# One layer of a hybrid decoder on one core: time steps in four row groups, the query scale on the scores, a later table load, and early short transfers in the weights' queue

## The chip, the cores and the metric

The kernel runs on one core of one Trainium2 chip. The metric is device microseconds of one execution, the median of several runs. The engines of the core are TensorE (PE), VectorE (DVE), ScalarE (ACT), GpSimd (POOL) and SyncE (SP, which only issues transfers). A core has 16 DMA engines, fed by queues that SP, ACT and POOL issue into.

## What is computed

One inference step of one layer, in fp32, for 256 prompt tokens and 64 sample tokens (8 sequences of 8), which share all weights; the model is 2048 wide. Cut to its skeleton:

```python
x += mixer(rmsnorm(x))         # h = xn @ w_in, split into z, x/B/C, dt, sc_h, sc_b, sc_c
                               # dt = softplus(h_dt + dt_bias); a = -exp(a_log) * dt   (32 heads)
                               # x/B/C: causal conv of 4 taps, silu; ssd_scan; short conv of 3 taps
                               # out = concat(y_ssd * silu(z) normed, y_sc) @ w_out
x += mem_attend(rmsnorm(x), k, v)   # k, v = rmsnorm(mem) @ w_mem_k, w_mem_v for the prompt; cached for samples
x += peer(rmsnorm(x))
# peer: q = xn @ w_peer_q; s = q . sub_keys (8 heads, 2 halves, 128 keys)
#       top 16 of each half, top 16 of their 256 sums -> expert ids and softmax gates g
#       act = gelu(xn . u[eid]);  out = sum of g * act * v[eid]       (16384 experts)
y = rmsnorm(x)                 # and the new SSM, conv and memory states are returned
```

## The kernel before

The layer is a chain of matrix products whose weights come from HBM once. Every fp32 weight tile is split into two parts, a rounded H and the rest L (`split`, L246 to L249: ACT copies, DVE subtracts), and so are the tokens (AH, AL; BH, BL); three matmuls (AH x H, AL x H, AH x L) make one product. In the order of time: K and V of the memory tokens (`tokens_gemm`, matmuls L318 to L320), the columns of w_in (`gemm`, matmuls L371 to L373: first the 32 dt columns C_DT, then B, C, x, then the short convolution's), the z columns, w_out, attention over memory (L1196 to L1430), the query of the experts, then a sweep over all of peer_u (U stage, L1939 to L1993) and over all of peer_v (V stage, L2034 to L2146).

The order of the work on PE, ACT and DVE is the program's own order. The class `Stream` writes it: a weight unit is loaded (SP's queue, into one of four rooms of 512 KB, tiles named W), split into rings of seven H and L, and popped, which is when its matmuls are written. Side work (generators passed to `side`) takes a step after each pop, `soon(n, fn)` runs a function n pops later, and `wait(n)` lets n steps pass. The orders of SP and POOL come from a tile scheduler. A room is taken by a load, and given back when DVE has subtracted its second half. A copy of peer_u to a transposed tensor u_d in HBM goes on beside it, 1 MB at a time, in ACT's queue.

The places that are touched:

- `histories` (L537 to L551) loads, on POOL's queue at the program's start, dt_bias, a_log, the D row, and the convolutions' histories into HX, four row groups of 24 x 24 x 32 and four of 16 x 16 x 32 floats. `vectors` (L517) loads norm gains and convolution weights on SP's queue; `x_norm` (L490) normalises the tokens during the K/V stage.
- The dt columns come from `gemm(w_in[0], C_DT, NH, ...)`: four loads of 64 KB in weight rooms, eight units of six matmuls with 32 columns of PE in use. `evac_dt` adds the bias, and `delta` (L616) computes softplus by a series, on 32 partitions x 320 tokens (tiles dt, DTT, AT); after `wait(DW)`, `decays` (L647) turns DTT and AT by six transposes (`ptd`) into DN and AN, 128 tokens x 32 heads, and makes running sums (`pta`, `ptc`), their exponentials (DD) and `ptr`.
- `residual` (L1032) transposes x again in the z stage from tiles xr, and `short_in` (L1047) splits the short convolution's result from tiles ys; both load on POOL's queue.
- `norm_p` (L1549) makes rs, the reciprocal root mean square of each token, from a sum over partitions (`prs`), on all partitions and by token columns. `evac_p` (L1601) scales q by it on DVE and has ACT copy the sample columns a second time; `scores` (L1611) multiplies q with the keys (`psc` for prompt, `pscs` for samples), and ACT copies the scores to SS, from which `best_keys` (L1632 to L1640) takes the top 16 on DVE.
- In the U stage, an expert block's result `at` gets its Gelu on ACT (L1988) and goes to act_d on SP's queue. `open_v` (L2011) opens the V stage and runs a Sqrt on one column (`warm`, L2022), which makes ACT load that function's table.

Of the kernel before, what the change touches and what calls it, by code (L numbers as in the profile page):

```python
# [19 lines left out]
P = 128  # L20
# [27 lines left out]
DW, XW, LAG = 8, 5, 4  # L48
# [115 lines left out]
def step(ctx, tc, ins, outs, dbg=None, stop=None):  # L164
# [325 lines left out]
    def x_norm():  # L490
        gb = gain_rows(norm_mix[0])
        yield from wait(4)
# [44 lines left out]
    def histories():  # L537
        nc.gpsimd.dma_start(dtb, ssd_dt_bias[0].rearrange("(h o) -> h o", o=1))
        nc.gpsimd.dma_start(alog, ssd_a_log[0].rearrange("(h o) -> h o", o=1))
        heads_d = pM.tile([P, NH], F32, name="heads_d")  # L540
        nc.gpsimd.dma_start(heads_d, ssd_d[0].rearrange("(o h) -> o h", o=1).broadcast_to([P, NH]))
        G.memset(HX, 0.0)
        for c0, src, nrow, nk in ((0, state_ssd_conv, 24, 24), (768, state_short_conv, 16, 16)):
            rows = src[0].rearrange("b j (k r i) -> r (b j) k i", r=4, i=32)
            for r in range(4):
                nc.gpsimd.dma_start(HX[32 * r:32 * r + nrow, c0:c0 + 32 * nk].rearrange("c (k i) -> c k i", i=32), rows[r])
            yield 1
        for h2 in range(2):
# [67 lines left out]
    def delta(x, e, s, s2):  # L616
# [6 lines left out]
        yield 1  # L623
        V.tensor_tensor(s, s, e, ALU.mult)
        V.tensor_tensor(s2, s, s, ALU.mult)
        yield 1
        q = e
        V.tensor_scalar(q, s2, 1.0 / 17, None, op0=ALU.mult)
        for j in range(7, 0, -1):
            V.scalar_tensor_tensor(q, q, 1.0 / (2 * j + 1), s2, ALU.add, ALU.mult)  # L630
            if j % 2:
                yield 1
        V.scalar_tensor_tensor(q, q, 1.0, s, ALU.add, ALU.mult)
        V.tensor_scalar(x, x, 0.0, None, op0=ALU.max)
        yield 1
        V.scalar_tensor_tensor(DTT, q, 2.0, x, ALU.mult, ALU.add)
        V.tensor_scalar(AT, DTT, alog, -1.0, op0=ALU.mult, op1=ALU.mult)
        yield from wait(DW)
        yield from decays()

    def evac_dt(m, pt):
        d = pS.tile([P, 3, 512], F32, tag="XD", bufs=1, name="dt")[0:NH].rearrange("p a b -> p (a b)")
        d = [d[:, i * T:(i + 1) * T] for i in range(4)]
        V.tensor_scalar(d[0], pt[0:NH, 0:T], dtb, None, op0=ALU.add)
        strm.side(delta(*d), 1)

    def decays():  # L647

        pt = ps("ptd")
        for j, src in enumerate((DTT, AT)):  # L650
            for b in range(3):
                n = P if b < 2 else TS
                transpose(pt[0:n, (3 * j + b) * NH:(3 * j + b + 1) * NH], src[:, b * P:b * P + n])
        for j, dst in enumerate((DN, AN)):
            S.activation(dst[:, 0:2], pt[:, 3 * j * NH:(3 * j + 2) * NH].rearrange("p (b h) -> p b h", h=NH), AF.Copy)
            S.activation(dst[0:TS, 2], pt[0:TS, (3 * j + 2) * NH:(3 * j + 3) * NH], AF.Copy)
        yield from wait(2)
# [288 lines left out]
    gemm(w_in[0], C_DT, NH, AH, AL, T, evac_dt)  # L946
# [100 lines left out]
    def short_in():  # L1047
        for k in range(KC):
            y = pZ.tile([P, T], F32, tag="ys", bufs=3, name="ys")
            nc.gpsimd.dma_start(y, ysc_d[k])  # L1050
            split(BH[:, k], BL[:, k], y)
# [549 lines left out]
    def evac_p(m, pt, c):  # L1601
# [3 lines left out]
        V.tensor_tensor(q[:, 0:T], pt[:, 0:T], RS["p"], ALU.mult)  # L1605
        S.activation(q[:, T:T + TS], q[:, TP:T], AF.Copy)
# [4 lines left out]
    def scores(c, qs):  # L1611
# [8 lines left out]
        S.activation(PP["SS"][:, 0:2, 2 * c + 1:2 * c + 3], pt.rearrange("p (j t k) -> p t j k", t=2, k=P), AF.Copy)  # L1620
# [4 lines left out]
        S.activation(PP["SS"][:, 2, 2 * c + 1:2 * c + 3], pt[:, 0:2 * P].rearrange("p (j k) -> p j k", k=P), AF.Copy)  # L1625
# [297 lines left out]
    def u_unit(i, q):  # L1923
# [36 lines left out]
        def comp():  # L1960
# [18 lines left out]
            if q == 3:  # L1979
# [31 lines left out]
    def open_v():  # L2011
# [10 lines left out]
        S.activation(warm, ident[:, 0:1], AF.Sqrt)  # L2022
# [229 lines left out]
```

## Time and profile before

| | us |
|---|---|
| median of 3 runs | 3107.21 (3105.64 to 3111.11) |
| the profiled execution | 3115.06 |
| its span in the trace | 3113.4 |
| PE busy | 3063.9 (98%) |
| DVE busy | 2281.4 (73%) |
| ACT busy | 1588.7 (51%) |
| POOL busy | 1341.6 (43%) |

The span is the time from the first to the last instruction in the trace; 1.66 us of the profiled execution lie outside it. Busy shares are means over stages with different limits, so the places where an engine stands still are read one by one. Matmuls overlap in the records: the time of one is the distance from its start to the next one's start, not its duration. The clock column of the windows is the granted TensorE clock, 1.00 for 2.4 GHz and 0.50 for 1.2 GHz.

### The profile page before, as it was taken

Reading aid. Unit: us, or ns where it says so; the run is one execution under the profiler, and the core shown is the slowest. Engines: PE = TensorE matmul, PEld = TensorE weight load, DVE = VectorE, ACT = ScalarE, POOL = GpSimd, SP = SyncE. Lnnn points to the kernel's source line nnn. Section 1 sums busy time; section 2 is a strip of 40 time slices with the busy share of each in tenths; the row PEclk is TensorE's granted clock in tenths of the full one; section 3 lists DMA queues with packets and bytes.
Section 4 is the critical chain, followed back from the end, with each engine's and each line's share of the span. In section 5 each row is a group of like instructions: output and inputs, shape, how many; then the busy total and the mean of one; then the engine's idle time right before and its main releaser. Section 6 shows DMA issues by size and latency. Waiting matters only on the chain.

```text
span 3113.4 us, 55309 instructions
## 1 busy us (share of the span) xinstructions
PE 3063.9 (98%) x19685; PEld 2804.0 (90%) x19685; DVE 2281.4 (73%) x4500; ACT 1588.7 (51%) x3192; POOL 1341.6 (43%) x1509
## 2 busy tenths in 40 slices
PE   8999999999999999999999999999999999999998
PEld 7889999999999999889999999888888888877886
DVE  5556776666566456656888899988885878878886
ACT  5545544334454444344454444767665555544555
POOL 1011221111110002320358899988886546456543
PEclk9999999999999999999999999999999999999999
DMA  7888899899999858975866788879998999998996
GB/s 259 291 272 298 296 335 323 303 325 314 343 327 340 277 179 224 269 251 157 232 214 214 283 320 317 304 288 324 331 330 274 343 329 364 320 328 314 334 318 217
DMA packets 442025, 909.16 MB, mean 292 GB/s; under 512 B 39880, under 2 KB 248944, under 8 KB 416276
## 3 DMA queue, kind: packets, MB, share of 16 engines
q1 hardware_dynamic: 312980, 543.11, 51.3%
q0 software_dynamic: 61040, 227.77, 22.2%
q10 hardware_dynamic: 67728, 134.75, 12.7%
q8 instruction: 154, 2.52, 0.3%
q14 instruction: 123, 1.01, 0.1%
HBM read 849.41 MB, written 190.05 MB: 334 GB/s over the span
## 4 chain that ended last, share of the span: by engine, by line
PE 41%; DMA 2%; POOL 2%; DVE 2%; issue 2%; ACT 1%; DVEq 0%; SPq 0%; POOLq 0%; ACTq 0%
PE pu L1970 8%; PE acc L2145 6%; PE acc L2144 6%; PE acc L2146 6%; PE pu L1971 4%; PE pu L1977 2%; PE pu L1976 2%; PE pu L1975 2%; POOL L L1951 2%; PE pgate L1873 2%; DMA at<-act_d 1%; DMA gv<-in_peer_v_dram,EV 1%; DVE L L249 1%; PE pg L373 1%; PE pg L372 1%
## 5 line engine op out<-in xcount | busy, mean ns | idle before, releaser
L249 DVE TENSOR_TENSOR L<-W,H 128x512 fp32r<-128x512 f32 x1320 | 899.5, 706 | 367.1 <-ACT H L248 360.3
L248 ACT ACTIVATE H<-W 128x512 fp32r<-128x512 f32 x1320 | 798.2, 625 | 719.1 <-PE acc L2146 227.9
L1951 POOL TENSOR_TENSOR L<-tt,H 128x512 fp32r<-128x512 f32 x511 | 646.4, 1297 | 60.7 <-ACT H L1948 55.0
L371 PE MATMUL pg<-AH,H 128*128 128x320 f32 (+1 forms) x1872 | 587.7, 314 | 0.3 <-ACT H L248 0.3
L373 PE MATMUL pg<-AH,L 128*128 128x320 f32 (+1 forms) x1872 | 579.7, 310 | 3.2 <-DVE L L249 3.2
L372 PE MATMUL pg<-AL,H 128*128 128x320 f32 (+1 forms) x1872 | 579.3, 309 | 0.0
L2145 PE MATMUL acc<-L,wt 128*128 128x512 f32 x1024 | 400.0, 391 | 6.3 <-DVE L L249 6.3
L2144 PE MATMUL acc<-H,wt 128*128 128x512 f32 x1024 | 399.6, 390 | 2.2 <-DVE at L1984 2.2
L2146 PE MATMUL acc<-H,wt 128*128 128x512 f32 x1024 | 399.4, 390 | 0.0
L1948 ACT ACTIVATE H<-tt 128x512 fp32r<-128x512 f32 x512 | 308.8, 625 | 142.1 <-DVE tt L1939 113.0
L1939 DVE STREAM_TRANSPOSE tt<-W 128x512 f32<-128x512 f32 x512 | 337.8, 690 | 52.6 <-POOL L L1951 48.6
L1970 PE MATMUL pu<-XP,H 128*128 128x512 f32 x1035 | 371.3, 399 | 0.0
L373 PEld LDWEIGHTS pg<-AH,L 128*128 128x128 f32 (+1 forms) x1872 | 351.0, 188 | 4.8 <-DVE L L249 4.2
L371 PEld LDWEIGHTS pg<-AH,H 128*128 128x128 f32 (+1 forms) x1872 | 351.4, 188 | 3.1 <-ACT H L248 0.9
L372 PEld LDWEIGHTS pg<-AL,H 128*128 128x128 f32 (+1 forms) x1872 | 351.0, 188 | 2.4
L1971 PE MATMUL pu<-XP,L 128*128 128x256 f32 x1104 | 297.1, 279 | 0.2 <-POOL L L1951 0.2
L1977 PE MATMUL pu<-XP,L 128*128 128x256 f32 x944 | 268.9, 285 | 1.7 <-POOL L L1951 1.6
L1975 PE MATMUL pu<-XP,H 128*128 128x256 f32 x944 | 267.7, 284 | 0.0
L1976 PE MATMUL pu<-XP,H 128*128 128x256 f32 x944 | 267.0, 283 | 0.0
L2093 POOL TENSOR_TENSOR at<-at,G 128x108 f32<-128x108 f32 x192 | 151.5, 803 | 262.7 <-DMA at<-act_d 215.8
L2145 PEld LDWEIGHTS acc<-L,wt 128*128 128x128 f32 x1024 | 192.9, 188 | 47.4 <-DVE L L249 7.3
L2144 PEld LDWEIGHTS acc<-H,wt 128*128 128x128 f32 x1024 | 192.9, 188 | 42.6 <-ACT wt L248 2.6
(495 smaller groups left out, 5817.0 us busy)
## 6 DMA issues: line engine op xcount, KB each, us to landing
u_d<-in_peer_u_dram ACTq DMA_DIRECT2D x128, 1024.0 KB
W<-u_d SPq DMA_DIRECT2D x128, 1024.0 KB
W<-in_peer_v_dram SPq DMA_DIRECT2D x256, 512.0 KB
W<-in_w_in_dram SPq DMA_DIRECT2D x176, 512.0 KB
W<-in_w_out_dram SPq DMA_DIRECT2D x64, 512.0 KB
W<-in_w_mem_k_dram SPq DMA_DIRECT2D x32, 512.0 KB
W<-in_w_mem_v_dram SPq DMA_DIRECT2D x32, 512.0 KB
kv<-in_cache_mem_k_dram POOLq DMA_DIRECT2D x64, 256.0 KB
```

The lines of the kernel that those rows point to most:

```text
L248: S.activation(h, src, AF.Copy)
L249: V.tensor_tensor(l, src, h.bitcast(F32), ALU.subtract)
L371: PE.matmul(out, hv[:, j, c0:c1], ah[:, k, 0:n], start=st, stop=False)
L372: PE.matmul(out, hv[:, j, c0:c1], al[:, k, 0:n], start=False, stop=False)
L373: PE.matmul(out, lv[:, j, c0:c1], ah[:, k, 0:n], start=False, stop=sp)
L1939: V.transpose(tt.rearrange("p (k a i) -> p k a i", a=4, i=32), box["x", i].rearrange("p (a k j) -> p k a j", a=4, k=16)[:, 4 * q:4 * q + 4])
L1951: G.tensor_tensor(l, src, h.bitcast(F32), ALU.subtract)
L1970: PE.matmul(*wide, start=k == 0, stop=False)
L1971: PE.matmul(pu[:, 0:TP], lv[:, j], PP["xp"][:, 0, k], start=False, stop=False)
L2144: PE.matmul(out, th, h, start=i == 0, stop=False)
L2145: PE.matmul(out, th, l, start=False, stop=False)
L2146: PE.matmul(out, tl, h, start=False, stop=i == P - 1)
```

## The change

The history loads, dt_bias and a_log go from POOL's queue to SP's, among the K/V weights, and the 2048 x 32 dt weights are loaded there whole (WDT, 128 x 16 x 32, rows of 128 bytes). The dt columns are then one unit without weight loads or splits: 32 fp32 matmuls with unrounded weights, of which four neighbours go to different column groups of 32 (k = 4q + j to group j), so that each group holds a part of the sum. FOLD (four stacked identities) adds the four parts and turns the result in one matmul per 128 tokens. `delta` then runs on 128 x 96, and `decays` starts without transposes, two steps later instead of eight. Residual rows are loaded one tile ahead (two buffers for xr), and the short convolution's one tile ahead. The query is copied unscaled on ACT; the scale becomes a per-partition operand of the score copies, for which rs is turned into a column (`prt`). `warm` is run 12 pops later, and the last two stores to act_d go through ACT's queue.

```diff
     def histories():
-        nc.gpsimd.dma_start(dtb, ssd_dt_bias[0].rearrange("(h o) -> h o", o=1))
-        nc.gpsimd.dma_start(alog, ssd_a_log[0].rearrange("(h o) -> h o", o=1))
...
-                nc.gpsimd.dma_start(HX[32 * r:32 * r + nrow, c0:c0 + 32 * nk].rearrange("c (k i) -> c k i", i=32), rows[r])
+                nc.sync.dma_start(HX[32 * r:32 * r + nrow, c0:c0 + 32 * nk].rearrange("c (k i) -> c k i", i=32), rows[r])
...
+    def dt_unit():
+
+        pt = ps("pdt")
+        for i, a in enumerate((AH, AL)):
+            for q in range(4):
+                for j in range(4):
+                    k = 4 * q + j
+                    PE.matmul(pt[32 * j:32 * j + 32, 0:T], WDT[:, NH * k:NH * k + NH], a[:, k].bitcast(F32),
+                              start=i == q == 0, stop=i == 1 and q == 3)
+        S.activation(D4[:, 0:T], pt[:, 0:T], AF.Copy)
+        strm.side(delta(), 1)
+
+    def delta():
+
+        yield from wait(2)
+        pt = ps("ptd")
+        for b in range(3):
+            PE.matmul(pt[:, b * NH:(b + 1) * NH], D4[:, b * P:(b + 1) * P], FOLD, start=True, stop=True)
...
+        V.tensor_tensor(by_block(x), by_block(pt[:, 0:3 * NH]), rows(DTB), ALU.add)
         V.scalar_tensor_tensor(e, x, -1.0, x, ALU.mult, ALU.max)
         S.activation(e, e, AF.Exp, scale=-1.0)
+        S.activation(ALOG, ALOG, AF.Exp)
...
-    gemm(w_in[0], C_DT, NH, AH, AL, T, evac_dt)
+    strm.add(None, None, None, dt_unit)
...
     def residual():
...
+                for src in (x_prompt[0, 0:P], x_prompt[0, P:TP]) if b == 0 else (x_sample.rearrange("b l d -> (b l) d"),):
+                    xts.append(pZ.tile([P, D], F32, tag="xr", bufs=2, name="xr"))
+                    nc.gpsimd.dma_start(xts[-1][:src.shape[0]], src)
...
     def norm_p():
...
+        yield from wait(3)
+        pt = ps("prt")
+        for i in range(2):
+            PE.matmul(pt[:, i:i + 1], r[:, i * P:(i + 1) * P], ident[:, 0:1], start=True, stop=True)
+            PE.matmul(pt[TS * i:TS * i + TS, 2:3], r[:, TP:T], ident[:, 0:1], start=True, stop=True)
+        RS["t"] = PP["pool"].tile([P, 3], F32, name="rt")
+        S.activation(RS["t"], pt[:, 0:3], AF.Copy)
...
-        V.tensor_tensor(q[:, 0:T], pt[:, 0:T], RS["p"], ALU.mult)
-        S.activation(q[:, T:T + TS], q[:, TP:T], AF.Copy)
+        S.activation(q[:, 0:TP], pt[:, 0:TP], AF.Copy)
+        S.activation(q[:, TP:].rearrange("p (r t) -> p r t", r=2), pt[:, TP:T].unsqueeze(1).broadcast_to([P, 2, TS]), AF.Copy)
...
-        S.activation(PP["SS"][:, 0:2, 2 * c + 1:2 * c + 3], pt.rearrange("p (j t k) -> p t j k", t=2, k=P), AF.Copy)
+        for tb in range(2):
+            S.activation(PP["SS"][:, tb, 2 * c + 1:2 * c + 3], pt.rearrange("p (j t k) -> p t j k", t=2, k=P)[:, tb], AF.Copy,
+                         scale=RS["t"][:, tb:tb + 1])
...
-                    nc.sync.dma_start(act_d[:, i], at)
+                    (nc.scalar if i >= P - 2 else nc.sync).dma_start(act_d[:, i], at)
...
-        S.activation(warm, ident[:, 0:1], AF.Sqrt)
+        strm.soon(12, lambda: S.activation(warm, ident[:, 0:1], AF.Sqrt))
```

How the instructions stand, at three places. First, the issues of short transfers at the start. On POOL before, after the masks (dtb, alog and heads_d are the three small vectors; XS holds HX):

```order
L538 DMA dtb<-in_ssd_dt_bias_dram 32x1
L500 AFFINE_SELECT TRI<-TRI 128x128
L504 AFFINE_SELECT BDO<-BDO 64x64
L539 DMA alog<-in_ssd_a_log_dram 32x1
L506 AFFINE_SELECT BDO<-BDO 64x64
L541 DMA heads_d<-in_ssd_d_dram 128x32
L542 MEMSET XS 128x1280
L546 DMA XS<-in_state_ssd_conv_dram 24x24x32 x4
L546 DMA XS<-in_state_short_conv_dram 16x16x32 x4
```

On SP in the change, among the loads of w_mem_k (XS<-in_w_in is WDT, the last group of XS rows is HX):

```order
L440 DMA gb<-in_norm_mix_dram 128x2048
L298 DMA W<-in_w_mem_k_dram 128x2x512 x4
L520 DMA XS<-in_w_in_dram 128x16x32
L298 DMA W<-in_w_mem_k_dram 128x2x512 x2
L522 DMA XS<-in_ssd_dt_bias_dram 128x32
L523 DMA XS<-in_ssd_a_log_dram 128x32
...
L552 DMA XS<-in_state_ssd_conv_dram 24x24x32
L298 DMA W<-in_w_mem_k_dram 128x2x512 x4
L552 DMA XS<-in_state_ssd_conv_dram 24x24x32
L298 DMA W<-in_w_mem_k_dram 128x2x512 x3
```

POOL keeps only heads_d; the histories stand one by one between weight loads. Second, the dt columns on PE, before:

```order
L320 MATMUL pg_1691<-H,ML 128x512
L371 MATMUL pg_1895<-AH,H 32x320
L372 MATMUL pg_1895<-AL,H 32x320
L373 MATMUL pg_1895<-AH,L 32x320
L371 MATMUL pg_1895<-AH,H 32x320
L372 MATMUL pg_1895<-AL,H 32x320
```

and in the change:

```order
L320 MATMUL pg_1692<-H,ML 128x512
L626 MATMUL pdt<-AH,XS 32x320 x16
L626 MATMUL pdt<-AL,XS 32x320 x16
L371 MATMUL pg_1928<-AH,H 128x320
L372 MATMUL pg_1928<-AL,H 128x320
```

The 48 matmuls of the dt columns (the first five are shown) have become 32, and the first B columns follow them. Third, ACT where the U stage ends, before:

```order
L1993 ACTIVATE at<-pu 128x256
L2022 ACT_TABLE_LOAD
L2022 ACTIVATE warm<-ident 128x1
L1988 ACT_TABLE_LOAD
L1988 ACTIVATE at<-at 128x256
L248 ACTIVATE H<-W 128x512 x3
L248 ACTIVATE wt<-at 128x256
L248 ACTIVATE H<-W 128x512
L1988 ACTIVATE at<-at 128x256
```

and in the change (L2016 is the Gelu):

```order
L2021 ACTIVATE at<-pu 128x256
L2016 ACTIVATE at<-at 128x256
L2017 DMA act_d<-at 128x256
L248 ACTIVATE H<-W 128x512 x3
L248 ACTIVATE wt<-at 128x256
L248 ACTIVATE H<-W 128x512
L2016 ACTIVATE at<-at 128x256
L2017 DMA act_d<-at 128x256
L248 ACTIVATE H<-W 128x512 x3
L248 ACTIVATE wt<-at 128x256
L248 ACTIVATE H<-W 128x512 x4
L2050 ACT_TABLE_LOAD
```

Both Gelus stand ahead of the table load, which is now one in place of two, and a store follows each of them on this engine.

## Rows read from the trace of the kernel before

**Rows 1.** the page, its first part (busy time, share of the span and instructions of each engine) and the first line of its fourth (the chain that ended last, shares of the span).

```profile
PE 3063.9 (98%) x19685; PEld 2804.0 (90%) x19685; DVE 2281.4 (73%) x4500; ACT 1588.7 (51%) x3192; POOL 1341.6 (43%) x1509
...
PE 41%; DMA 2%; POOL 2%; DVE 2%; issue 2%; ACT 1%; DVEq 0%; SPq 0%; POOLq 0%; ACTq 0%
```

**Rows 2.** the windows: for each stretch (us from the span's start) its length, then busy us (and instructions) of PE, PE's weight loads, DVE, ACT and POOL, the granted TensorE clock as a share of 2.4 GHz, the mean busy share of the DMA engines, and GB/s.

```profile
11.00:18.00 7.00, 7.00 (x29) 5.54 (x28) 1.58 (x3) 0.97 (x2) 0.61 (x3) 1.00 1.07 208
19.00:27.00 8.00, 4.88 (x12) 3.76 (x13) 5.34 (x10) 4.86 (x10) 0.00 (x0) 0.65 1.04 412
50.00:200.00 150.00, 150.00 (x678) 121.82 (x677) 84.15 (x143) 81.55 (x142) 7.61 (x14) 1.00 0.84 278
240.00:243.00 3.00, 3.00 (x13) 3.00 (x13) 2.46 (x5) 1.21 (x3) 0.00 (x0) 0.50 1.04 364
300.00:800.00 500.00, 499.72 (x3762) 486.44 (x3762) 342.05 (x743) 221.92 (x435) 93.29 (x208) 1.00 0.93 315
929.50:933.00 3.50, 3.50 (x15) 3.50 (x15) 1.78 (x3) 2.29 (x5) 0.00 (x0) 0.54 0.96 327
1537.20:1539.40 2.20, 2.20 (x10) 2.20 (x9) 1.88 (x4) 0.85 (x3) 1.20 (x3) 0.50 0.60 157
2400.70:2403.60 2.90, 2.90 (x8) 2.30 (x7) 2.13 (x4) 0.97 (x2) 0.50 (x1) 0.50 1.19 344
```

**Rows 3.** the timeline of ACT and of PE around 20 us: start us, us, engine, line, operation, written<-read, and in brackets the idle time before it and what ended it.

```profile
19.85 1.85 ACT L248 ACTIVATE H<-W 128x512 fp32r<-128x512 f32 x3 [7.87 <-DMA W<-in_w_mem_k_dram]
...
22.12 0.80 PE L318 MATMUL pg<-H,MH 128*128 128x512 f32 x1 [3.57 <-ACT MH L281]
```

**Rows 4.** the DMA issues from 0 to 30 us: written<-read, issuing queue, count, KB each.

```profile
XS<-in_state_ssd_conv_dram POOLq DMA_DIRECT2D x4, 72.0 KB
```

**Rows 5.** the waits from 50 to 200 us, of SP's queue and of ACT: who waited for whom, us in total, times, longest us.

```profile
SPq L298 <- DVE L L249: 112.1, 48, 7.0
...
ACT H L248 <- DMA W<-in_w_mem_v_dram: 5.0, 2, 2.5
```

**Rows 6.** the timeline of PE, the first matmul of the dt columns and the first behind them.

```profile
203.66 0.31 PE L371 MATMUL pg<-AH,H 128*32 128x320 f32 x1
...
210.71 0.32 PE L371 MATMUL pg<-AH,H 128*128 128x320 f32 x1
```

**Rows 7.** the timeline of PE in the attention stage: two runs of 16 fp32 matmuls in four column groups, each with the matmul behind it.

```profile
1303.67 0.64 PE L1390 MATMUL pss<-tt,qm 128*32 128x128 f32 x16
1304.24 0.41 PE L1196 MATMUL pg<-BH,H 128*128 128x320 f32 x1
...
1352.82 1.92 PE L1430 MATMUL pso<-kv,pm 128*32 128x512 f32 x16
1354.67 0.34 PE L241 MATMUL ppt<-ident,SN 64*128 64x64 f32 x2
```

**Rows 8.** the waits of PE from 200 to 262 us.

```profile
PE pg L373 <- DVE L L249: 3.2, 4, 1.9
PE ptr L686 <- DVE DD L673: 1.2, 1, 1.2
PE pg L371 <- ACT H L248: 0.3, 1, 0.3
```

**Rows 9.** the groups of DVE by form from 218 to 240 us (line, engine, operation, shapes, count | busy us, mean ns | idle us before), and one line of ACT's timeline.

```profile
L630 DVE SCALAR_TENSOR_TENSOR dt<-dt 32x320 f32<-32x320 f32 x7 | 3.3, 477 | 0.1
L622 DVE RECIPROCAL dt<-dt 32x320 f32<-32x320 f32 x1 | 2.1, 2141 | 0.0
...
254.50 1.28 ACT L672 ACT_TABLE_LOAD   x1
```

**Rows 10.** the waits of PE from 800 to 935 us, and ACT's timeline at the first W_out weights.

```profile
PE pg L371 <- ACT H L248: 1.5, 1, 1.5
PE pt L241 <- DMA xr<-in_x_prompt_dram: 0.8, 1, 0.8
PE pg L373 <- DVE L L249: 0.2, 1, 0.2
...
927.31 1.15 ACT L248 ACTIVATE H<-W 128x512 fp32r<-128x512 f32 x2 [4.90 <-DMA W<-in_w_out_dram]
```

**Rows 11.** the waits of PE from 1495 to 1545 us, and DVE's timeline between the sum of squares and the first use of rs.

```profile
PE psc L1618 <- DVE q L1605: 2.5, 2, 2.1
...
1474.55 0.49 DVE L265 TENSOR_SCALAR ms<-prs 128x320 f32<-128x320 f32 x1 [0.46 <-PE prs L263]
...
1479.70 0.55 DVE L1577 SCALAR_TENSOR_TENSOR xn<-XN,GAIN,rs 128x320 f32<-128x320 f32 x1
```

**Rows 12.** the timeline of ACT and of PE where the U stage ends and the V stage begins.

```profile
2394.03 1.28 ACT L2022 ACT_TABLE_LOAD   x1
...
2396.83 0.42 ACT L1988 ACTIVATE at<-at 128x256 f32<-128x256 f32 x1
...
2396.99 0.39 PE L2146 MATMUL acc<-H,wt 128*128 128x512 f32 x1
2399.57 0.47 PE L2144 MATMUL acc<-H,wt 128*128 128x512 f32 x1 [2.19 <-DVE at L1984]
```

**Rows 13.** the timeline of PE in the V stage, its two longest pauses.

```profile
2770.91 0.50 PE L2145 MATMUL acc<-L,wt 128*128 128x512 f32 x1 [2.75 <-DVE L L249]
...
2855.00 0.79 PE L2145 MATMUL acc<-L,wt 128*128 128x512 f32 x1 [3.53 <-DVE L L249]
```

More of the change, by code (lines that the diff above doesn't have):

```diff
@@ L47 @@
 R_SSD, R_BEST, R_CHOOSE, R_CHOOSE2, R_OUT = 0.7, 0.6, 0.40, 0.32, 0.29
-DW, XW, LAG = 8, 5, 4
+XW, LAG = 5, 4
 AIN, AHEAD, HOT, G2B = 2, 1, 2, 3
@@ L490, in x_norm @@
     def x_norm():
+        yield from wait(2)
         gb = gain_rows(norm_mix[0])
-        yield from wait(4)
+        yield from wait(2)
         for b in range(2):
@@ L614, in step, with by_block, rows @@
     strm.then(open_s)
-    def delta(x, e, s, s2):
+    def dt_unit():
[9 more added lines that the diff above has]
+    def delta():
+        yield from wait(2)
+        pt = ps("ptd")
+        for b in range(3):
+            PE.matmul(pt[:, b * NH:(b + 1) * NH], D4[:, b * P:(b + 1) * P], FOLD, start=True, stop=True)
+        scratch = pS.tile([P, 3, 512], F32, tag="XD", bufs=1, name="dt").rearrange("p a b -> p (a b)")
+        x, e, s, s2 = (scratch[:, 3 * NH * i:3 * NH * (i + 1)] for i in range(4))
+        def by_block(t):
+            return t.rearrange("p (b h) -> p b h", h=NH)
+        def rows(t):
+            return t.unsqueeze(1).broadcast_to([P, 3, NH])
+        V.tensor_tensor(by_block(x), by_block(pt[:, 0:3 * NH]), rows(DTB), ALU.add)
         V.scalar_tensor_tensor(e, x, -1.0, x, ALU.mult, ALU.max)
         S.activation(e, e, AF.Exp, scale=-1.0)
+        S.activation(ALOG, ALOG, AF.Exp)
         yield 1
@@ L630, in delta @@
             V.scalar_tensor_tensor(q, q, 1.0 / (2 * j + 1), s2, ALU.add, ALU.mult)
-            if j % 2:
-                yield 1
+        yield 1
         V.scalar_tensor_tensor(q, q, 1.0, s, ALU.add, ALU.mult)
         V.tensor_scalar(x, x, 0.0, None, op0=ALU.max)
[L635 to L638, printed above, removed]
+        V.scalar_tensor_tensor(DN, by_block(q), 2.0, by_block(x), ALU.mult, ALU.add)
+        V.scalar_tensor_tensor(AN, DN, -1.0, rows(ALOG), ALU.mult, ALU.mult)
+        yield from wait(2)
         yield from decays()
[L641 to L645, printed above, removed]
-    def decays():
[L649 to L657, printed above, removed]
+    def decays():
         pt = ps("pta")
@@ L1047, in short_in @@
     def short_in():
[L1048 to L1051, printed above, removed]
+        ys = []
+        for k in range(KC + 1):
+            if k < KC:
+                ys.append(pZ.tile([P, T], F32, tag="ys", bufs=3, name="ys"))
+                nc.gpsimd.dma_start(ys[k], ysc_d[k])
+            if k:
+                split(BH[:, k - 1], BL[:, k - 1], ys[k - 1])
             yield 1
@@ L1624, in scores @@
             PE.matmul(pt[:, j * P:(j + 1) * P], q[:, TP:TP + P], PP["KY"][:, 2 * c + j], start=True, stop=True)
-        S.activation(PP["SS"][:, 2, 2 * c + 1:2 * c + 3], pt[:, 0:2 * P].rearrange("p (j k) -> p j k", k=P), AF.Copy)
+        S.activation(PP["SS"][:, 2, 2 * c + 1:2 * c + 3], pt[:, 0:2 * P].rearrange("p (j k) -> p j k", k=P), AF.Copy,
+                     scale=RS["t"][:, 2:3])
         done.add(("score", c))
```

28 lines of the change are left out of this document (15 added, 13 removed).

## The prediction

> **What bounds the kernel now.** I read the page first, then the windows by stage, then every wait of TensorE, and last what its releaser had waited for. The page puts PE at 98% of the span, and the chain that ended last runs over PE more than over anything else [rows 1]: PE's own program is the bound. In the long W_in stretch PE is busy 499.72 of 500 us, in the K/V stretch 150.00 of 150 [rows 2]. So there are two ways to gain: fewer PE cycles, or removing the few places where PE stands still. After each longer pause PE also runs on at granted clock 0.50 (1.2 GHz) for 2 to 5 us [rows 2]; half of such a stretch is lost as well, and I count it with its pause. The change aims at six such places. They come in time order below.
>
> The profiled execution took 3115.06 us: 3113.4 of span and 1.66 outside. It is 7.85 us above the median of the runs. I make the sum against 3115.06 and carry the difference over to the median.
>
> **Start, 11 to 28 us.** PE stands 3.57 us before L318 at 22.12. ACT (MH) is named, but ACT itself had idled 7.87 us for a K/V weight load before the H at 19.85 and works in order [rows 3]. From 11 to 18 us, DMA moves 208 GB/s at a busy share of 1.07; from 19 to 27 us 412 GB/s [rows 2]. What is different is the eight history loads on POOL's queue (four of 72 KB [rows 4], four smaller), whose rows are 32 floats long (128 bytes, L545). In seven microseconds some 1.4 MB went, which at 412 GB/s takes 3.5: the weight load comes 3.5 us sooner at least, about the pause. With the pause goes the half clock: PE has 4.88 us busy in the window 19 to 27 at a granted 0.65, and the part after 22.12 is at 0.50, so 2.4 lost. Available 3.57 + 2.4 = 6.0; taken 5.5, bounds 0 (something else in that queue was slow) and 6.0.
>
> The history loads, and now a 2048-run load of WDT, go into SP's queue among the K/V weights. Behind each of them stands the next weight load, and ACT's split of it, DVE's, and PE. The cover: SP's weight loads wait 112.1 us, 48 times, for a room to be freed by DVE, while ACT waits on V weights only 5.0 us [rows 5], and the stretch's DMA share is 0.84 [rows 2]. The queue is ahead of its readers, so I put the cost at 0.7 us; without that cover it is the first rival.
>
> **dt columns, 204 to 211 us.** 48 matmuls on 32 columns of PE run from 203.66 to 210.71: 7.05 us [rows 6]. They become 32 fp32 matmuls in eight groups of four, each four in different column groups. Four-group matmuls of this form exist: 16 of 128 columns take 1303.67 to 1304.24, 0.143 us a group; 16 of 512 columns take 1352.82 to 1354.67, 0.463 a group [rows 7]. Scaled to 320 columns by the first that is 0.356 a group, 2.85 in all; by the second 0.289, 2.3 in all. I take 2.5, nearer the longer row: saved 4.5 us. If the groups did not overlap, 32 x 0.289 = 9.2, a loss of 2.2. Three small matmuls (FOLD) replace six transposes: nothing.
>
> A group of other shape needs no extra term: the two rows run from the first start to the next ordinary matmul, so what entering and leaving the form costs is in them. The Trainium skill (TensorEngine Tiling (Array Packing), Key Properties) says that a change of tiling mode drains TensorE, which speaks against this step. The rows show none beyond what they contain; if the rule added the length of one ordinary matmul (7.05 / 48 = 0.147 us) at each end, the saving would be 4.2 in place of 4.5.
>
> **Delta and first B tiles, 211 to 262 us.** PE waits here 3.2 + 1.2 + 0.3 = 4.7 us [rows 8], and the window 240 to 243 is at clock 0.50, 1.5 more: 6.2. Two causes. The four dt loads hold rooms that the first B loads then lack, and they go. And DVE runs the delta on 32 x 320: seven steps of 0.477, a reciprocal of 2.141 [rows 9], and eight more steps, counted at 0.477 too: 9.3 us between L splits. On 128 x 96 the elements in a row are 0.3 of that: between 2.8 us (all by length) and 9.3 (all fixed cost); I take 4.5. The Exp table load of 1.28 us that stood before the first DD [rows 9] moves ahead into delta, under weight units. New risk: PE takes `pta` 48 matmuls (7.0 us) after the FOLD matmuls, and the chain between (1.28 of table, 4.5 of DVE, some L splits) is about as long, so up to 1.5 us may come back. Taken: 4.5 of 6.2, bounds 0 and 6.2.
>
> **z stage, 800 to 933 us.** 0.8 us is a wait for xr, asked for sooner now. 1.5 + 0.2 us stand at the first W_out weights, with 0.54 of clock for 3.5 us, 1.6 more [rows 2, 10]. There ACT waited for DMA [rows 10]; the new pool layout holds some cache loads back, so fewer share the queue with those weights, but later. Available 4.1; taken 1.5, bounds -1.5 (the same burst later) and 4.1.
>
> **Peer query, 1475 to 1545 us.** PE waits 2.5 us for q, which DVE scales behind a block of top-16 steps [rows 11], and the window at 1537 is at half clock, 1.1 more [rows 2]. ACT now copies q from PSUM (51% busy over the span [rows 1]), so PE no longer stands behind DVE; scale goes onto score copies that DVE reads later. Taken 3.4 of 3.6, bounds 1.5 and 3.6. Four tiny matmuls turn rs into a column: rs is ready at about 1479.70 when its first reader starts. PE is at them 36 matmuls (5.3 us) and four transposes after the sum, 1474.55 [rows 11], near 1480.2: no wait, by 0.5 us; 0.3 of cost.
>
> **U to V, 2397 us.** ACT loads a table for `warm` at 2394.03 and the Gelu one again; Gelu starts at 2396.83, and PE pauses from 2396.99 on for 2.19 us until DVE has used it [rows 12]. Then 2.9 us at 0.50, 1.45 more [rows 2]. With `warm` behind the last Gelu, Gelu comes 2396.83 - 2394.03 = 2.80 us sooner, more than the pause. ACT's two loads then lie where weights are split ahead. Taken 3.4 of 3.6, bounds 1.5 and 3.6. The last two stores go to ACT's queue, an issue each: nothing. The Trainium skill (ScalarE: Activation LUTs, What ACT_TABLE_LOAD costs) gives about 2.66 us for each switch, so two would be 5.3; the rows show 2.80 for both with the work between. The pause caps the gain either way.
>
> **Sum.** 5.5 + 4.5 + 4.5 + 1.5 + 3.4 + 3.4 = 22.8, less 0.7 and 0.3, rounded: 21.5. Profiled: 3115.06 - 21.5 = 3093.6. Median: 3107.21 - 21.5 = 3085.7, say 3086. The upper bounds together (6.0, 4.75, 6.2, 4.1, 3.6, 3.6) give 28: 3079. Of weak ends at several places at once (2, 4, 1.5, 0, 2, 2) 11.5: 3096.
>
> **Rivals.**
> 1. The queue gives part of it back. Small-run loads that slowed the start now delay K/V weights, WDT first, where rings are still filling. For it: the 208 GB/s. Against it: the 112.1 us that SP waits for rooms. Two stalls of 2 us with half clock, 2.4 each: 8.8 back, 3095. Chance 0.20. The Trainium skill (DMA: Bandwidth & Descriptors, Specifications) asks for 512 bytes or more for line rate; the windows agree in kind, 208 against 412.
> 2. Stalls that the change does not touch move. Late in V, PE waits 2.75 and 3.53 us for L [rows 13] behind data-bound work of DVE. They depend on where transfers stand when PE comes, some 20 us sooner. Gone: 6.3 and a half clock, 3078; one more pair: 3093. Chance 0.12, half each way.
> 3. The four groups do not overlap: 4.5 + 2.2 worse, 3092. Chance 0.04.
> 4. Slower than before. The K/V stretch has 16% of 150 us free, 24 us of 16 engines. 4 x 24 x 24 + 4 x 16 x 16 = 3328 short runs of the histories and 2048 of WDT use it up if each holds an engine 71 ns (24 x 16 / 5376); from there on weights come late. If a run holds as long as the weights' 2048-byte ones, they weigh like 11 MB, at 278 GB/s 40 us: 16 too much. With four stalls at half clock (2.4 each) and the start's 5.5 not gained: 3086 + 16 + 9.6 + 5.5 = 3117. Against it: 412 to 208 GB/s for 7 us at the start is a loss of some 3.5 us for most of these runs, a tenth of the 40. Chance 0.04.
>
> **How the numbers follow.** The forecast, with every cover as named, has 0.60: 3079 to 3092, 3086 likeliest. Range: 3077 to 3097, which leaves out rival 4, the far half of the first (a third stall), and part of the lower half of the second. What a measurement of this kernel tells from no change is about 0.2%, 6 us: faster is below 3101, slower above 3113.4. All of the forecast, rivals 2 and 3 and most of rival 1 lie below 3101: 0.89. Rival 1 with three stalls, or several small ends at once, 0.07 within. Slower 0.04.
>
> **What would show it.** Right: no ACT wait of 8 us for a weight near 20 us, and PE at clock 1.00 from 20 to 28; the `pdt` matmuls over in 2.3 to 2.9 us; no half clock near 240; no wait of psc for q; no Gelu table load at the U to V switch. Wrong: PE waits between 20 and 200 us (rival 1), above all with ACT waiting for W; `pdt` over 4.5 us (rival 3); a wait at `pta` over 1.5 us; a new pause in 930 to 960; late V pauses that are other than 2.75 and 3.53.

## The result and the profile after

The changed kernel takes 3090.54 us (median of 18 runs, 3082.28 to 3105.76) where the kernel before, in 18 runs beside it, takes 3107.11 (3102.64 to 3112.49): a ratio of 0.9946, 95% interval 0.9938 to 0.9954, so 0.54% or 16.6 us faster. 3086 was forecast from 3107.21, 21 us. The profiled execution of the changed kernel took 3088.27 us, 1.77 of it outside the span. Spans alone differ by 26.9 us, so part of that belongs to these two executions; both kernels were profiled a second time below.

The page of the changed kernel, its span and first part, answers to [rows 1]:

```profile
span 3086.5 us, 55315 instructions
PE 3051.7 (99%) x19709; PEld 2794.0 (91%) x19709; DVE 2275.2 (74%) x4477; ACT 1589.5 (51%) x3202; POOL 1359.7 (44%) x1500
```

PE is busy 12.2 us less (a matmul at half clock counts as busy for longer), and the span is 26.9 shorter: more than half of the gain is standing still that is gone. The windows of the changed kernel, columns as in [rows 2]:

```profile
11.00:18.00 7.00, 7.00 (x26) 5.56 (x25) 4.38 (x8) 4.03 (x8) 0.00 (x0) 1.00 1.03 417
19.00:27.00 8.00, 8.00 (x45) 6.64 (x44) 6.24 (x12) 5.31 (x12) 0.00 (x0) 1.00 0.91 277
800.00:935.00 135.00, 135.00 (x923) 133.27 (x922) 86.21 (x150) 73.80 (x139) 16.15 (x28) 1.00 1.01 340
```

DMA moves 417 GB/s from 11 to 18 us instead of 208, and PE runs at clock 1.00 from 19 to 27. From 800 to 935 it never stands. The waits of PE that are left at the other places, from 195 to 262, 1460 to 1600 and 2370 to 2385 us (who waited for whom, us in total, times, longest):

```profile
PE pta L670 <- DVE AN L663: 0.6, 1, 0.6
...
PE pu L2005 <- POOL L L1979: 1.1, 1, 1.1
...
PE acc L2172 <- DVE at L2012: 1.1, 1, 1.1
```

They answer to [rows 8, 11, 12]: 4.7 us has become 0.6, the 2.5 for q is gone, 2.19 at the switch is 1.1. The second row is new. And PE's dt columns, in the timeline:

```profile
199.26 2.36 PE L626 MATMUL pdt<-AH,XS 128*32 128x320 f32 x32
201.44 2.34 PE L626 MATMUL pdt<-AL,XS 128*32 128x320 f32 x32
203.70 0.42 PE L371 MATMUL pg<-AH,H 128*128 128x320 f32 x1
```

From 199.26 to 203.70 is 4.4 us, where 2.5 was forecast. The two counts of 32 belong to 16 matmuls each.

Where the time went is best seen by cutting each trace at PE's own marks (last matmul of K/V; first of B; first of W_out; first and last of attention, pss and pso; last pscs; first and last acc). The table has the distance from one mark to the next in us, from matmul starts in the timelines, for the two profiles of each kernel.

| stretch | before | before again | after | after again |
|---|---|---|---|---|
| start to the end of K/V | 203.4 | 202.8 | 198.9 | 200.9 |
| to the first B matmul (dt) | 7.3 | 7.3 | 4.8 | 4.8 |
| to the first W_out matmul | 717.3 | 716.7 | 707.6 | 707.2 |
| to the first pss | 260.4 | 260.1 | 258.3 | 264.1 |
| attention, to the last pso | 184.7 | 186.6 | 187.1 | 186.9 |
| to the last pscs | 233.1 | 233.2 | 229.3 | 229.8 |
| to the first acc (U stage) | 786.3 | 786.4 | 788.7 | 789.4 |
| V stage | 708.4 | 702.7 | 699.2 | 699.3 |
| to the end of the span | 12.5 | 12.5 | 12.6 | 12.8 |

The means of the two differ by 19.9 us: 3.2 at the start, 2.5, 9.6, -1.0, -1.3, 3.5, -2.7, 6.3 and -0.2.

### The profile page after: what moved, and what is told of

Read it like the earlier page. It is cut to its first block, busy times and chain, and to the rows that moved or that the text cites. A ratio compares the mean times of both kernels' runs of the same rounds, so it can differ in the third digit from the quotient of the medians.

```text
span 3086.5 us, 55315 instructions
## 1 busy us (share of the span) xinstructions
PE 3051.7 (99%) x19709; PEld 2794.0 (91%) x19709; DVE 2275.2 (74%) x4477; ACT 1589.5 (51%) x3202; POOL 1359.7 (44%) x1500
## 3 DMA queue, kind: packets, MB, share of 16 engines
q10 hardware_dynamic: 68016, 135.01, 12.8%
## 4 chain that ended last, share of the span: by engine, by line
PE 84%; issue 4%; DMA 3%; POOL 3%; DVE 3%; ACT 1%; SPq 0%; DVEq 0%; POOLq 0%; ACTq 0%
PE pg L371 11%; PE pg L372 11%; PE pg L373 11%; PE pu L1998 7%; PE acc L2173 6%; PE acc L2174 6%; PE acc L2172 6%; PE pu L1999 4%; POOL L L1979 3%; PE pu L2005 2%; PE pu L2004 2%; PE pu L2003 2%; PE pgate L1901 2%; PE pg L1214 2%; PE pg L319 1%
## 5 line engine op out<-in xcount | busy, mean ns | idle before, releaser
L371 PE MATMUL pg<-AH,H 128*128 128x320 f32 x1856 | 581.7, 313 | 0.0
L373 PE MATMUL pg<-AH,L 128*128 128x320 f32 x1856 | 573.6, 309 | 0.0
L372 PE MATMUL pg<-AL,H 128*128 128x320 f32 x1856 | 573.4, 309 | 0.0
L371 PEld LDWEIGHTS pg<-AH,H 128*128 128x128 f32 x1856 | 349.0, 188 | 2.1 <-issue 0.5
L372 PEld LDWEIGHTS pg<-AL,H 128*128 128x128 f32 x1856 | 348.7, 188 | 1.8
L373 PEld LDWEIGHTS pg<-AH,L 128*128 128x128 f32 x1856 | 348.4, 188 | 0.0
L2121 POOL TENSOR_TENSOR at<-at,G 128x108 f32<-128x108 f32 x192 | 168.4, 891 | 252.0 <-DMA at<-act_d 205.0
L1998 PEld LDWEIGHTS pu<-XP,H 128*128 128x128 f32 x1035 | 194.3, 188 | 39.9
```

Of the source, the lines that this page charges most:

```text
L371: PE.matmul(out, hv[:, j, c0:c1], ah[:, k, 0:n], start=st, stop=False)
L372: PE.matmul(out, hv[:, j, c0:c1], al[:, k, 0:n], start=False, stop=False)
L373: PE.matmul(out, lv[:, j, c0:c1], ah[:, k, 0:n], start=False, stop=sp)
L1998: PE.matmul(*wide, start=k == 0, stop=False)
```

## The experiments

Each alters the changed kernel by the lines shown, but for the two copies; `...` marks lines left out. Medians are of six runs where an interval is given, single runs otherwise.

**Histories on POOL's queue again.** (hist_pool)

```diff
-                nc.sync.dma_start(HX[32 * r:32 * r + nrow, c0:c0 + 32 * nk].rearrange("c (k i) -> c k i", i=32), rows[r])
+                nc.gpsimd.dma_start(HX[32 * r:32 * r + nrow, c0:c0 + 32 * nk].rearrange("c (k i) -> c k i", i=32), rows[r])
```

> The changed kernel with the eight history loads back on POOL's queue at the start; WDT, dt_bias and a_log stay among the K/V weights. Theory (the histories' short rows starve the first weight loads): ACT waits 7 to 8 us for a K weight near 20 us, PE stands about 3.5 us at 18 to 22 us and runs at half clock until 27, the last K/V matmul comes 4.5 us later than the changed kernel's 198.93, at 203 to 204, nothing else changes, time 3094 to 3096. Rival (the start is slow for another cause, such as the order of the token loads): the last K/V matmul within 1 us of 198.93, time as the changed kernel, 3090.

Measured: 3093.36 us, ratio to before 0.9947 (0.9933 to 0.9961); the time cannot be told from the changed kernel's. The trace can. Windows and ACT's timeline of this kernel:

```profile
11.00:18.00 7.00, 6.50 (x17) 4.64 (x17) 2.31 (x5) 2.03 (x5) 0.00 (x0) 1.00 1.05 193
19.00:27.00 8.00, 5.58 (x28) 4.09 (x27) 3.46 (x8) 3.50 (x7) 0.00 (x0) 1.00 1.02 388
```

```profile
17.11 1.15 ACT L248 ACTIVATE H<-W 128x512 fp32r<-128x512 f32 x2 [4.18 <-DMA W<-in_w_mem_k_dram]
...
22.37 1.83 ACT L248 ACTIVATE H<-W 128x512 fp32r<-128x512 f32 x3 [4.10 <-DMA W<-in_w_mem_k_dram]
```

193 GB/s and eight microseconds of ACT's waiting for weights are back, in two parts, and the last K/V matmul comes at 208.6, 7.8 and 9.7 us later than in the two profiles of the changed kernel. The cause at the start is shown; the rival falls. The size, larger than the 4.5 expected, says less: this profiled execution (3103.58 us) is the slowest of its six, its first K/V matmul came 1.1 us later than the changed kernel's, and a pause of 2.9 us near 62 us is in it. One more thing differs from the kernel before: the change also asks for the gain rows gb (SP's queue) later, at 9.05 us where it was 7.03. This kernel does so too and starves all the same, so that was not the cure.

**All dt matmuls in one column group.** (dt_one_group)

```diff
-                PE.matmul(pt[32 * j:32 * j + 32, 0:T], WDT[:, NH * k:NH * k + NH], a[:, k].bitcast(F32),
+                PE.matmul(pt[0:32, 0:T], WDT[:, NH * k:NH * k + NH], a[:, k].bitcast(F32),
...
```

> The changed kernel with all 32 dt matmuls in one column group of 32 instead of four; the other three groups of D4 are zero. The dt matmuls of the changed kernel take 4.1 us, 0.13 each, where 2.5 was forecast. Theory (an fp32 matmul costs four times its columns, which the rows of before hid because each is recorded twice, and the four groups overlap fully): 4 x 4.1 = 16.5 us, 0.53 each. Rival (two passes only, and the groups overlap by half): 8.5 us. No time is asked of it, only the trace.

Measured, PE's timeline of this kernel (single run 3107.41):

```profile
198.44 8.80 PE L624 MATMUL pdt<-AH,XS 128*32 128x320 f32 x32
207.08 8.78 PE L624 MATMUL pdt<-AL,XS 128*32 128x320 f32 x32
215.79 0.42 PE L371 MATMUL pg<-AH,H 128*128 128x320 f32 x1
```

17.35 us for the same 32 matmuls, 3.9 times the 4.44 (not 4.1) of four groups: 0.54 us each. The groups overlap almost fully, as the forecast had it; the price of one is what it had wrong. The program has 64 pso matmuls and 256 pss where the trace has 128 and 512 records: an fp32 matmul leaves two. So each row of 16 in [rows 7] was 8 matmuls, two rounds of four groups and not four rounds, and a round costs twice what I read.

**Query scaled on DVE again.** (q_on_dve)

```diff
-        S.activation(q[:, 0:TP], pt[:, 0:TP], AF.Copy)
+        V.tensor_tensor(q[:, 0:T], pt[:, 0:T], RS["p"], ALU.mult)
+        S.activation(q[:, T:T + TS], q[:, TP:T], AF.Copy)
...
```

> The changed kernel with the query scaled on DVE again, without the rs column and the scaled score copies. Theory: psc waits for q behind the top-16 steps again, 2.5 us and a half clock stretch worth 1.1; from the second prs matmul to the last pscs matmul 132 us in place of 128.4; time 3093 to 3095. Rival (PE simply comes at another phase and the wait would have gone anyway): 128.4 within 1 us, no wait of psc above 0.5.

Measured: 3095.41 us, ratio 0.9949 (0.9933 to 0.9964), as the changed kernel within the interval. PE's waits of this kernel from 1480 to 1530 us:

```profile
PE psc L1636 <- DVE q L1623: 2.5, 2, 2.1
```

The same wait returns to the tenth, and the stretch from the last prs matmul to the last pscs is 132.1 us, as in the kernel before; the changed kernel has 128.4. Shown. Not all of it is kept in every execution: of the eleven traces with q on ACT, five show a wait of 0.4 to 1.2 us for ACT in its place, none of them among the changed kernel's own two. The longest, from stores_sp below:

```profile
1530.31 1.16 PE L1643 MATMUL psc<-KY,q 128*128 128x128 f32 x8 [1.19 <-ACT q L1630]
```

Over those eleven the stretch is 128.4 to 129.9 us.

**Table load and stores as before at the V switch.** (warm_early)

```diff
-        strm.soon(12, lambda: S.activation(warm, ident[:, 0:1], AF.Sqrt))
+        S.activation(warm, ident[:, 0:1], AF.Sqrt)
-                    (nc.scalar if i >= P - 2 else nc.sync).dma_start(act_d[:, i], at)
+                    nc.sync.dma_start(act_d[:, i], at)
```

> The changed kernel with the Sqrt for the table back at the opening of V and both late stores of act_d on SP. Theory: two table loads stand between the two Gelus, PE pauses 2.2 us or more at the switch in place of 1.14, half clock behind it worth 1.4; from the first acc matmul on the V stage is 2.5 us longer near its start; time 3092 to 3094. Rival (what is left of the pause, 1.14 us, is set by PE's distance to DVE and not by the tables): the pause stays within 0.5 us of 1.14.

Measured: 3089.68 us, ratio 0.9935 (0.992 to 0.995). ACT's timeline of this kernel, and PE's:

```profile
2381.75 1.28 ACT L2050 ACT_TABLE_LOAD   x1
2383.26 1.28 ACT L2016 ACT_TABLE_LOAD   x1
2384.55 0.42 ACT L2016 ACTIVATE at<-at 128x256 f32<-128x256 f32 x1
```

```profile
2387.29 0.77 PE L2172 MATMUL acc<-H,wt 128*128 128x512 f32 x1 [3.18 <-DVE at L2012]
```

The pause is 3.18 us with both tables loaded ahead of the Gelu, and V takes 702.3 us, 3.0 more. The cause is shown in the trace; the median is no higher than the changed kernel's, where 3092 to 3094 was expected.

**The z stage's loads as before** (z_old: `residual` and `short_in` of the kernel before, one xr buffer):

```diff
-                    xts.append(pZ.tile([P, D], F32, tag="xr", bufs=2, name="xr"))
...
+            xt = pZ.tile([P, D], F32, tag="xr", bufs=1, name="xr")
...
```

> The changed kernel with the residual rows and the short convolution's rows loaded as before (one xr buffer, no load ahead). Theory (the pool layout and the earlier requests cleared the pause at the first W_out weights): from the first B matmul to the first W_out matmul 3.9 us more than the changed kernel's 707.6, with a wait for xr of 0.8 and one of 1.5 or more at the first W_out unit; time 3094. Rival (that pause came of where the transfers stood when PE arrived, and went with the earlier changes): 707.6 within 1.2 us, only the xr wait of 0.8 returns, time 3090 to 3092.

Measured: 3089.6 us, ratio 0.9945 (0.9928 to 0.9962). Waits of PE from 800 to 960 us, of this kernel:

```profile
PE pg L371 <- ACT H L248: 1.1, 1, 1.1
PE pg L373 <- DVE L L249: 0.4, 2, 0.2
```

From the first B to the first W_out matmul it is 708.75 us, 1.1 to 1.6 more than the changed kernel (707.8 in the later experiment with the same loads), and not the 3.9 of the theory; the wait for xr that both sides expected is not there either. The w_in matmuls are the same in all these kernels, so the stretch can be cut at one of them, the one at 798.3 us in the profile of before. From it to the first W_out matmul PE takes 129.7 and 129.3 us before, 127.2 in all ten traces with the new loads, 128.8 here, and 127.9 in the later experiment. So the new loads give 0.6 to 1.6 of the 2.3 us gained there, and the rest came of other edits.

**The last two stores on SP's queue.** (stores_sp)

```diff
-                    (nc.scalar if i >= P - 2 else nc.sync).dma_start(act_d[:, i], at)
+                    nc.sync.dma_start(act_d[:, i], at)
```

> The changed kernel with the last two stores to act_d on SP's queue as before, the late table load kept. In the changed kernel ACT spends some 0.8 us on each store's wait and issue at 2377 and 2382, ahead of the splits that DVE's product of the last block stands behind. Theory (those 0.8 us are what is left of the pause): the PE pause at the switch falls from 1.14 to 0.5 or less, time 0.5 to 1 below the changed kernel. Rival (the store on SP's queue holds weight loads up behind it): a longer pause, or a new wait for a V weight in the first 20 us of V, 1 to 3 us longer.

Measured: 3089.07 us, ratio 0.9945 (0.9928 to 0.9961). ACT's timeline of the changed kernel, and PE's of this one:

```profile
2377.31 0.41 ACT L2016 ACTIVATE at<-at 128x256 f32<-128x256 f32 x1
2377.75 0.36 ACTq L2017 DMA_DIRECT2D act_d<-at  x1
2378.16 1.67 ACT L248 ACTIVATE H<-W 128x512 fp32r<-128x512 f32 x3 [0.44 <-ACT at L2016]
```

```profile
2378.03 0.47 PE L2172 MATMUL acc<-H,wt 128*128 128x512 f32 x1 [0.35 <-DVE at L2012]
```

In the changed kernel that matmul stands at:

```profile
2380.82 0.47 PE L2172 MATMUL acc<-H,wt 128*128 128x512 f32 x1 [1.14 <-DVE at L2012]
```

From the Gelu (2377.31) to it are 3.51 us. Here the Gelu is at 2375.29 and it is 2.74, as in the kernel before [rows 12] and in warm_early (2384.55 to 2387.29). So the store, which I had costed at nothing, costs 0.77 us of PE's time. V takes 697.9 us in place of 699.2, a difference that scatter covers: 697.4 to 706.3 over the eight traces with the stores on ACT's queue.

**Both kernels once more.** (after_again, before_again)

> The changed kernel once more, for its trace alone. In the first profile the V stage took 699.2 us from first to last acc matmul, 9.2 less than in the profile of before, of which the switch explains 2.5; the medians differ by 16.6, the profiles by 26.9. Theory (late pauses in V, which the change does not touch, come and go from run to run): V takes 700 to 710 here, and the stages ahead of V agree with the first profile within 1 us each. Rival (the change itself shortened V): 699 within 1 us again.

> The kernel before once more, for its trace alone. Theory (as for the changed kernel): its V stage differs from 708.4 by some us, 702 to 709, and the pauses at 2768 and 2851 are at other places or gone; the stages ahead of V agree within 1 us each. Rival: 708.4 within 1 us, the same two pauses.

Measured: the table above. V of the changed kernel was 699.3 us again, which I had not expected, while V of the kernel before went from 708.4 to 702.7, with one pause near 2850 in place of two:

```profile
2849.58 0.50 PE L2145 MATMUL acc<-L,wt 128*128 128x512 f32 x1 [2.31 <-DVE L L249]
```

The stages ahead did not agree within 1 us: in the changed kernel K/V and the stretch after W_out did not, in the kernel before attention. PE's timeline of its second profile:

```profile
56.94 0.51 PE L319 MATMUL pg<-L,MH 128*128 128x512 f32 x1 [2.52 <-DVE L L249]
...
925.07 0.78 PE L263 MATMUL prs<-acc,ones 128*128 128x320 f32 x2 [1.57 <-DVE acc L277]
...
937.11 0.41 PE L373 MATMUL pg<-BH,L 128*128 128x320 f32 x1 [2.17 <-DVE L L249]
```

These pauses, near 55 and near 930 us, are in neither profile of before with this length.

**Old z loads and stores on SP's queue together.** (z_old_stores) The two edits above.

> The changed kernel without two of its parts: the z stage's loads as before (one xr buffer, nothing asked ahead) and the last two act_d stores on SP's queue. Theory (the z part clears 1.1 to 1.5 us at the first W_out weights and moves its burst of cache loads into the w_out stage, where five of seven profiles with it show a pause of 1.5 to 3.6 us near 930 that the one without it lacks; the stores cost 0.8 us on ACT): from the first W_out matmul to the first pss 259 to 260 us again, with no pause over 1 us between 915 and 960; the switch pause at or under 0.5; time 1 to 3 us below the changed kernel, 3087 to 3089. Rival (the pause near 930 comes and goes with the phase of the transfers, whatever the layout): a pause over 1.5 us there in this profile too, time 3090.

Measured: 3090.76 us, ratio 0.9945 (0.993 to 0.9961): as the changed kernel and the rival. The theory's marks in the trace are there: no pause over 1 us from 915 to 960, 259.7 us from W_out to pss, and no pause of PE at the switch. From the first B matmul to the first pss the two kernels with the old loads take 967.5 and 968.1 us; nine traces with the new ones (the last experiment's among them, delta_slow left out, since its B stretch is altered) 965.5 to 966.0 four times, 967.3 once, and 970.3 to 971.7 four times. New loads gain some 2 us or lose some 3; what decides which is not shown.

**The dt weights loaded late.** (wdt_late)

```diff
     def vectors():
-        nc.sync.dma_start(WDT.rearrange("p (k h) -> p k h", h=NH),
-                          w_in[0][:, C_DT:C_DT + NH].rearrange("(k p) h -> p k h", p=P))
...
     def histories():
...
+        V.memset(WDT, 0.0)
+        nc.sync.dma_start(WDT.rearrange("p (k h) -> p k h", h=NH),
+                          w_in[0][:, C_DT:C_DT + NH].rearrange("(k p) h -> p k h", p=P))
```

> The changed kernel with the load of the dt weights (2048 rows of 128 bytes) held back to the end of the histories, near the end of the K/V stage; it is cleared once on DVE before. Theory 1 (the short rows at 22 to 25 us took the weights' lead, and PE's new pause near 54 us of 0.8 to 3.2 us pays for it): no pause over 0.5 us between 45 and 65 us, K/V from first to last matmul 188 to 189 us in place of 189 to 192. Theory 2 (the pause comes of the token rows and the K stores, 3 MB at 45 to 56 us, which PE now reaches 4 us sooner with less lead): the pause stays, 0.8 to 3 us, K/V 189 to 191.

Measured: 3084.97 us, one run. K/V took 188.2 us from its first matmul on, and the pause was 0.45 us:

```profile
56.53 0.50 PE L319 MATMUL pg<-L,MH 128*128 128x512 f32 x1 [0.45 <-DVE L L249]
```

That fits theory 1. But the first K/V matmul came at 10.72 us here, and K/V ended at 198.88 as in the changed kernel. z_old_stores, with the early load and a first matmul at 10.74, had a pause of 0.63 and took 188.8 us from there; wdt_stores below, with the late load and a first matmul at 10.63, 0.78 and 188.8. In the eight other traces with the histories on SP's queue that matmul came at 8.36 to 9.74, and the pause was 0.81 to 2.93. So the pause goes with PE's first wait, and the place of this load is not seen to matter. What makes the pause stays open: hist_pool lost its time at the start as the kernel before did, and has it all the same.

**More DVE work in delta.** (delta_slow)

```diff
...
+        V.reciprocal(idle, idle)
...
+        for j in range(7):
+            V.scalar_tensor_tensor(idle, idle, 1.0, idle, ALU.mult, ALU.mult)
```

> The changed kernel with idle DVE work put into delta: one reciprocal and seven steps on 32 x 320 beside the real ones on 128 x 96, 5.5 us more, so that delta costs DVE what it cost before or a little more; the results are not used. Theory 1 (DVE's series made PE wait at 217 to 262 us in the kernel before): 2 to 4 us of new PE waits between 205 and 250, from the first B matmul to the first W_out matmul 711 us or more in place of 707.2. Theory 2 (the lack of rooms and the late B loads behind the dt loads were the cause): one wait of pta, 3 to 5 us later than now since it needs AN, and none behind it for L splits; what follows pta within 1 us of 707.2 plus that wait. If the wait of pta is the whole, the two are told apart by the waits of pg for L between 217 and 250: present by the first, absent by the second.

Measured: one run 3099.62; from the first B to the first W_out matmul 715.55 us. PE's waits from 200 to 262 us, and the window behind the wait:

```profile
PE pta L675 <- DVE AN L668: 5.8, 1, 5.8
...
224.20:229.30 5.10, 5.10 (x22) 4.84 (x22) 1.81 (x7) 0.96 (x6) 0.00 (x0) 0.50 0.37 103
```

One wait, none of pg for L; with the half clock behind it (0.50 for 5.1 us, 2.6 lost) it makes up the 8 us. DVE's series alone did not bring the old waits back, which speaks for the rooms and late B loads; yet the pause of 5.8 us gave the weights time, so theory 1 is weakened, not excluded. The trace of the kernel before shows both ahead of PE's wait for L that ends at 224.39:

```profile
217.32 0.63 ACT L248 ACTIVATE H<-W 128x512 fp32r<-128x512 f32 x1 [8.57 <-DMA W<-in_w_in_dram]
...
221.65 2.14 DVE L622 RECIPROCAL dt<-dt 32x320 f32<-32x320 f32 x1
223.72 0.62 DVE L249 TENSOR_TENSOR L<-W,H 128x512 fp32r<-128x512 f32 x1
```

ACT stood 8.57 us for a late load, and then the L that PE needed stood behind the reciprocal. The changed kernel has no such wait of ACT from 200 to 236 us.

**Late dt weights and stores on SP's queue.** (wdt_stores)

> The changed kernel with the dt weights' load held back to the end of the K/V stage and the last two act_d stores on SP's queue: the two single edits whose traces looked best, put together. Theory (both remove a cost that the change brought): the last K/V matmul at 198 or before, no pause over 0.5 us near 55, V from first to last acc matmul 697 to 698; time 3085 to 3087, below the changed kernel's 3090.5. Rival (the K/V stage ends at 198 to 199 wherever that load stands, since what PE gains at the start it waits for near 55, and the run-to-run spread of V and of the w_out stage is larger than what the stores give): 3088 to 3091, the same as the changed kernel.

Measured: 3087.46 us, ratio 0.9927 (0.9912 to 0.9942). K/V ended at 199.5, the pause near 55 was 0.78, and V took 698.7: all three miss the theory's figures, and the rival's 198 to 199 is the nearer. The time lies between the theory's range and the rival's. It is the fastest median of six runs, but its interval overlaps the changed kernel's.

## Why the prediction was right

The sign, the range (3077 to 3097) and the causes held; the size was 16.6 of 21.5 in the medians, 19.9 by the traces. (The terms add up to 21.8.) That it came so near is in part luck: steps that came out too small and too large offset each other, and 5.6 of the 19.9 us are late pauses in V that no step counted; 14.3 would be left without them. By its steps:

- **Start**, 5.5 less 0.7: 3.2 in the traces. Cause shown by hist_pool. 1.3 us are lost ahead of the first K/V matmul, which came at 9.74 and 9.72 us where it was 8.45 and 8.46; over the eleven traces with the histories in SP's queue it comes at 8.36 to 10.74, so these runs do not tell that from scatter. From that matmul on K/V is 4.5 us shorter. Rival 1 took part of it: a wait for L near 55 us, none in either profile of before, stands in all eleven (0.45 to 2.93 us), and in hist_pool near 62 us (2.9), so it is not the histories' own; the 0.7 was too small for it.
- **dt columns**, 4.5: 2.5. This step failed in its size. "16 of 512 columns" [rows 7] were 16 records of 8 matmuls; with 0.93 us a round of 512 columns, eight of 320 would have been 4.6, against 4.4 measured.
- **Delta and z stage**, 4.5 and 1.5: 7.3 ahead of the w_in matmul at 798.3 us of before and 2.3 behind it, where 6.2 and 4.1 were counted as available. I had discounted both for waits that might return; pta cost 0.6. The delta step gave more than was counted as available; where the rest comes from is open, and so is how the step divides between DVE's shorter series and free rooms. Of the z stage's 2.3 the loads gave 0.6 to 1.6.
- **The burst of cache loads** (bound -1.5): PE does stand near 930 us in some executions; from W_out to pss these kernels take 258.3 to 264.5 us, against 260.1 and 260.4 before, so +2 to -4. That it is the cache loads is not shown. On the mean the z edit is worth nothing that these runs can show.
- **Peer query**, 3.4 less 0.3: 3.5. Shown by q_on_dve.
- **U to V**, 3.4: about 0.8. This step failed in its size too. In its first 40 us V loses 4.0 and 1.8 us in the profiles of before (the pause of 2.19 is 1.56 in the second), 1.4 and 2.9 in the changed kernel's. Of 2.19 us of pause 1.1 stayed, through the store that I had costed at nothing; with the stores on SP's queue and the late table load the loss is 0.4 to 0.6 in three traces.
- **Rival 2** was partly at work on the good side: late V pauses of before, 8.2 and 4.6 us lost by the two profiles, are 1.5 and 0.2 in those of the changed kernel (start-to-start distances beyond the usual, from 40 us behind the first acc on). q_on_dve, with 9.2 lost so and V of 706.3, shows that they can return.
- **Not foreseen**: the U stage takes 2.4 to 3.0 us more, 2.3 to 2.4 of it in its first 14 us. PE waits 1.1 us at pu for POOL, whose L stands in order behind a store x2s_d; ACT's next copy waits for the store before it to land, 6.2 us where it was 4.05. Why it lands later is open. The stage takes 787.6 us in q_on_dve and 788.2 to 789.9 in the eleven traces with q on ACT, so part of what the peer step gains may be lost here.

Of the signs named beforehand, four were against the forecast: `pdt` took 4.44 us and not 2.3 to 2.9, PE waits between 20 and 200 us, the second profile has a pause that ends at 937 us, and the late V pauses are others than before. The rest were as forecast.

Every single undoing leaves a median within 5 us of the changed kernel's, and a ratio whose interval holds the changed kernel's 0.9946; what is called shown rests on the traces, in which the undone part's own pause comes back.

## What to carry to other kernels

Count a matmul's records against the program before pricing it. Short-row transfers belong where the weight queue waits for room, not where it fills its first rooms. A store that is issued by the engine that makes its data is not free when a matmul waits behind that engine. And new waits may stand further on, as near 55 us and at the start of U here, both unexplained, while old ones go that no step aimed at: cut two traces of each kernel at the same matmuls before a gain is put down to a step.

## What the runs showed of the hardware

An fp32 matmul with 32 of 128 columns in use took 0.54 us on 320 columns (17.35 us for 32), where one of the rounded kind took 0.147 (7.05 us for 48, [rows 6]); four of them in different column groups took 0.55 together (4.44 us for eight groups). An fp32 matmul leaves two records in the trace (64 for the 32 of the dt columns). With a transfer issued from ACT right behind the Gelu that makes its data, ACT's next split began 0.85 us behind the Gelu's start (2377.31, 2378.16); with the transfer on SP's queue 0.31 us (2375.29, 2375.60).
